# The final norm taken by token, on rows turned ahead of the norm

## The chip, the core and the metric

One core of one Trainium2 chip runs the kernel. TensorE multiplies matrices into PSUM (eight banks of 128 partitions by 512 fp32), VectorE and ScalarE work on PSUM and SBUF, SyncE and ScalarE issue the transfers used here. The metric is the device time of one execution in microseconds (us); runs are compared by their median.

## The reference

A decoder layer on 512 tokens of width 1024: a SwiGLU feed-forward block, a token mixer (gMLP gating and a Mamba-2 scan), a second feed-forward block, a gated per-layer embedding, and a final norm, all fp32. The change lies in the last two steps:

```python
def rmsnorm(x, g):
    xf = x.astype(jnp.float32)
    y = xf * lax.rsqrt(jnp.mean(xf * xf, axis=-1, keepdims=True) + EPS)
    return (y * g.astype(jnp.float32)).astype(x.dtype)
...
        h = h + 0.5 * swiglu(rmsnorm(h, ffn2_norm[i]), ffn2_w_gate[i], ffn2_w_up[i], ffn2_w_down[i])
        gate = jax.nn.sigmoid(rmsnorm(h, ple_norm[i]) @ ple_w_gate[i] + ple_b_gate[i])
        h = h + gate * (p[i] @ ple_w_proj[i])
    return rmsnorm(h, final_norm)
```

## The kernel before

The residual `h` is kept as 8 tiles of 128 features (on the partitions) by 512 tokens, `h[0]` to `h[7]`. A product of fp32 operands is made in three passes: `weights(src, n)` loads 1024 columns of weights (`raw`), ScalarE casts them to fp32r (`whi`), VectorE subtracts to get the rest (`wlo`), and `accumulate` multiplies `whi` and `wlo` with the two parts of the activations `x`, 8 x 3 matmuls for each tile of 128 outputs.

The last stage has one such unit for each d from 0 to 7, called here the product of d. Units 0 to 4 are multiplied with all 512 tokens; units 5, 6 and 7 (`BY_HALF = 3`) with the first 256 tokens and the last 256 separately (`gate_half`). The norm's factor `r` for the tokens comes from the sums of squares of `h` (matmuls with `ones`, a root by Newton steps on VectorE, `diagonals`, and `spread`, a matmul that copies the factor to all partitions; `kept` is ScalarE's copy of it). `gate` then makes four steps for each d: a multiply by `r` (VectorE, from PSUM), a sigmoid (ScalarE), a multiply by the embedding tile `emb[d]` (VectorE), an add to `h[d]` (VectorE). After it each `h[d]` is squared (ScalarE; VectorE for d = 7), the full-width squares are added into `total`, and `gained` multiplies `h[d]` by the final norm's vector, one number for each feature, that is for each partition.

The output wants tokens on rows. For each half of the tokens `factors` sums the squares with matmuls by `ones` and takes the root (`rsqrt_by_table`: ScalarE's Sqrt, VectorE's reciprocal and one Newton step), and `rows_out` turns `h` by 128 x 128 transposes into PSUM, four to a tile (a tile holds 128 tokens by 512 features), scales each tile by the token's factor into `o` and stores it: ScalarE scales the first 512 features, VectorE the other 512, eight stores of 256 KB in all.

The program is recorded first and issued in an order that is written out by hand: `ORDER` is a list of unit numbers, where a unit is one instruction, or the matmuls in a row into one PSUM tile. Every engine works through its own instructions in this order, and waits for others by semaphores. PSUM tiles come from seven banks of the tag `b` and one of `a`. In the profile nearly all instructions carry the line of the call that issues them (L1905), so rows are told apart by tile names.

The part of `ORDER` that concerns the end lists TensorE's work as: the products of d = 1 and 0 (full), the sums, d = 2, the spread, d = 4, 5 (first half), 3, 5 (second half), 6 (first, second), 7 (first, second), the ones products of the first half, four of the turned tiles, the ones products of the second half, four turned tiles.

Of the kernel before, what the change touches and what calls it, by code (L numbers as in the profile page):

```python
# [27 lines left out]
ALU = mybir.AluOpType  # L28
# [24 lines left out]
    "m": 33, "convin": 2, "o": 8, "sq": 4,  # L53
}
REGION = dict.fromkeys(("raw0", "s0", "embt", "F", "xfa", "xfb", "x", "xa", "xb", "r4", "u", "emb"), "left") | dict.fromkeys(
    ("rawb", "whix", "wlox", "s1", "rawd", "ghi", "glo", "g", "u2", "p7", "m", "convin", "o", "sq"), "right",
# [15 lines left out]
    ("ple_b_gate", 8), ("final_norm", 8), ("d_skip", 8),  # L72
# [4 lines left out]
for _name, _w in _VECS:  # L77
# [211 lines left out]
def layer_kernel(ctx: ExitStack, tc: tile.TileContext, a: dict, out: bass.AP):  # L289
# [96 lines left out]
    def tmp():  # L386
        return sb("tmp")
# [1410 lines left out]
    def gate(d, ps, tok, engine):  # L1798

        t = tmp()[:, tok]  # L1800
        nc.vector.tensor_tensor(t, ps[:, tok], r[:, tok], ALU.mult)
        nc.scalar.activation(t, t, AF.Sigmoid, bias=col("ple_b_gate", d))
        engine.tensor_tensor(t, t, emb[d][:, tok], ALU.mult)
        engine.tensor_tensor(h[d][:, tok], h[d][:, tok], t, ALU.add)
        sq = tmp() if tok is whole else sb("sq", (P, half))
        if d < ND - 1:
            nc.scalar.activation(sq, h[d][:, tok], AF.Square)
        else:
            nc.vector.tensor_tensor(sq, h[d][:, tok], h[d][:, tok], ALU.mult)
        return sq  # L1810

    def gained(d, tok):

        if d < ND - 1:
            nc.scalar.activation(h[d][:, tok], h[d][:, tok], AF.Copy, scale=col("final_norm", d))
        else:
            nc.vector.tensor_scalar(
                h[d][:, tok], h[d][:, tok], col("final_norm", d), None, ALU.mult
            )

    total = sb("ssum")

    def done(d, ps):
        sq = gate(d, ps, whole, nc.vector)
        if d == 0:
            nc.vector.tensor_copy(total, sq)
        else:
            nc.vector.tensor_tensor(total, total, sq, ALU.add)
        gained(d, whole)

    for d in range(ND - BY_HALF):
        ps = mm_ps()
        accumulate(ps, weights(a["ple_gate"][d], D), 0, x)
        if d == 0:
            tok, first = norm.per_token(D), ps
            continue
        if d == 1:
            r = Norm.on_all(tok)
            done(0, first)
        done(d, ps)  # L1840
    units = [weights(a["ple_gate"][d], D) for d in range(ND - BY_HALF, ND)]
    def gate_half(i, tok):
        d = ND - BY_HALF + i
        ps = sm_ps()
        accumulate(ps[:, tok], units[i], 0, x, tokens=tok)
        sq = gate(d, ps, tok, nc.vector)
        gained(d, tok)
        return sq

    def factors(tok, sqs):  # L1850

        chunks = range(tok.start // P, tok.stop // P)
        ps = sm_ps()
        for j, sq in enumerate([total[:, tok]] + sqs):
            for i in range(len(chunks)):
# [157 lines left out]
```

## Time and profile before

| | |
|---|---|
| median of 3 runs | 1073.28 us (1072.68 to 1074.14) |
| profiled execution | 1073.36 us, of which the span is 1071.6 us |
| granted TensorE clock, mean over the span | 0.999 |
| TensorE matmuls busy | 1062.1 us (99% of the span) |
| VectorE busy | 817.0 us (76%) |
| ScalarE busy | 559.5 us (52%) |
| GpSimd busy | 75.2 us (7%) |
| HBM traffic | 161 GB/s over the span |

Times in the views count from the span's start. A row of the timeline has the start, the duration, the engine (PE is TensorE, PEld its weight load, DVE VectorE, ACT ScalarE, SP SyncE; a q behind the name is the engine's queue of DMA issues), the line, the operation, what it writes <- what it reads, shapes, and how many are merged (x3); in brackets stands how long the engine was idle before it, and what ended the wait.

### The profile page before, as it was taken

How to read it: one execution, taken by the hardware profiler on the slowest of the kernel's cores; microseconds unless marked ns; L12 is line 12 of the kernel's file. 1: busy time of each engine (PE TensorE's matmuls, PEld its weight loads, DVE VectorE, ACT ScalarE, POOL GpSimd, SP SyncE). 2: the span in 40 equal slices, each digit the busy share in tenths (PEclk: the TensorE clock that was granted, in tenths of full speed). 3: DMA queues.
4: the chain of work that ended last, by engine and by line, in shares of the span. 5: the costliest groups of instructions: out<-in, count | busy, mean ns of one | idle time of the engine just before them, and what ended most of it. 6: DMA issues, size and time to landing. Idle time of an engine off the chain costs nothing.

```text
span 1071.6 us, 17611 instructions
## 1 busy us (share of the span) xinstructions
PE 1062.1 (99%) x7151; PEld 965.0 (90%) x7151; DVE 817.0 (76%) x1169; ACT 559.5 (52%) x781; POOL 75.2 (7%) x95
## 2 busy tenths in 40 slices
PE   9999999999999999999999999999999999999997
PEld 7899999999998878998999888999999999999887
DVE  6978685867577879999999767988667575857866
ACT  7655344444444537887865435654434343534545
POOL 1100000100000000000100000010100000000000
PEclk9999999999999999999999999999999999999999
DMA  9876765766452236777855435786755757633412
GB/s 322 238 202 166 196 181 193 196 181 174 99 154 82 65 113 146 187 201 175 212 135 130 138 98 137 218 236 186 204 143 155 211 144 197 181 115 85 139 53 79
DMA packets 52209, 173.27 MB, mean 162 GB/s; under 512 B 5920, under 2 KB 6176, under 8 KB 52128
## 3 DMA queue, kind: packets, MB, share of 16 engines
q1 hardware_dynamic: 33696, 116.93, 32.1%
q0 software_dynamic: 12256, 44.57, 23.1%
q10 hardware_dynamic: 6176, 10.65, 3.4%
q8 instruction: 56, 0.92, 0.3%
q14 instruction: 25, 0.20, 0.1%
HBM read 167.86 MB, written 4.26 MB: 161 GB/s over the span
## 4 chain that ended last, share of the span: by engine, by line
PE 99%; DVE 0%; ACT 0%; issue 0%; DVEq 0%; ACTq 0%
PE b L1905 81%; PE a L1905 18%; DVEq L2008 0%; DVE o L1905 0%; ACT m L1905 0%; ACT b L1905 0%; DVE tmp L1905 0%; DVE h L1905 0%; DVE ones L410 0%; DVE nv L1905 0%; ACTq L1905 0%
## 5 line engine op out<-in xcount | busy, mean ns | idle before, releaser
L1905 PE MATMUL b<-xfb,whi 128*128 128x256 f32 (+1 forms) x1704 | 297.5, 278 | 0.7 <-ACT b L1905 0.7
L1905 PEld LDWEIGHTS b<-xfb,whi 128*128 128x128 f32 x1704 | 261.0, 188 | 6.0 <-ACT b L1905 0.9
L1905 PE MATMUL b<-xfb,wlo 128*128 128x256 f32 (+1 forms) x852 | 237.2, 278 | 0.0
L1905 ACT CAST whi<-raw 128x1024 fp32r<-128x1024 f32 (+1 forms) x131 | 136.0, 1041 | 146.4 <-PE b L1905 109.7
L1905 DVE TENSOR_TENSOR wlo<-raw,whi 128x1024 fp32r<-128x1024 f32 (+1 forms) x130 | 156.8, 1212 | 28.7 <-ACT whi L1905 25.8
L1905 PEld LDWEIGHTS b<-xfb,wlo 128*128 128x128 f32 x852 | 159.9, 188 | 0.5
L1905 PE MATMUL b<-xfa,whi 128*128 128x256 f32 (+1 forms) x696 | 124.0, 281 | 0.0
L1905 PEld LDWEIGHTS b<-xfa,whi 128*128 128x128 f32 x696 | 107.0, 188 | 2.5 <-DVE xfa L1905 0.2
L1905 PE MATMUL b<-xfa,wlo 128*128 128x256 f32 (+1 forms) x348 | 97.8, 281 | 0.0
L1905 ACT CAST whix<-rawd 128x1024 fp32r<-128x1024 f32 (+1 forms) x40 | 39.4, 986 | 88.5 <-PE a L1905 47.9
L1905 DVE TENSOR_TENSOR wlo<-rawb,whi 128x1024 fp32r<-128x1024 f32 x51 | 62.1, 1220 | 23.2 <-ACT whi L1905 23.1
L1905 ACT CAST whi<-rawb 128x1024 fp32r<-128x1024 f32 x51 | 53.3, 1049 | 48.8 <-PE b L1905 39.7
L1905 PE MATMUL b<-m,whi 128*128 128x512 f32 x224 | 69.6, 392 | 0.0
L1905 DVE TENSOR_TENSOR wlox<-rawd,whix 128x1024 fp32r<-128x1024 f32 (+1 forms) x40 | 45.7, 1143 | 27.0 <-ACT whix L1905 26.9
L1905 PEld LDWEIGHTS b<-xfa,wlo 128*128 128x128 f32 x348 | 65.4, 188 | 0.5
L1905 PE MATMUL b<-xb,whi 128*128 128x256 f32 (+1 forms) x280 | 62.2, 318 | 0.0
L1905 PE MATMUL b<-ghi,wlox 128*128 128x512 f32 x156 | 61.4, 394 | 0.0
L1905 PE MATMUL b<-glo,whix 128*128 128x512 f32 x156 | 61.2, 392 | 0.0
L1905 PE MATMUL b<-ghi,whix 128*128 128x512 f32 x156 | 60.7, 389 | 0.0
L1905 PE MATMUL a<-ghi,wlox 128*128 128x512 f32 x140 | 55.2, 394 | 0.0
L1905 PE MATMUL a<-glo,whix 128*128 128x512 f32 x140 | 54.9, 392 | 0.0
L1905 PE MATMUL a<-ghi,whix 128*128 128x512 f32 x140 | 54.4, 389 | 0.0
(294 smaller groups left out, 2223.8 us busy)
## 6 DMA issues: line engine op xcount, KB each, us to landing
raw<-in_ffn_gu SPq DMA_DIRECT2D x57, 512.0 KB, 5.4
rawd<-in_ffn_down SPq DMA_DIRECT2D x40, 512.0 KB, 4.4
raw<-in_ffn_gu POOLq DMA_DIRECT2D x32, 512.0 KB, 7.7
rawb<-in_ffn_gu SPq DMA_DIRECT2D x31, 512.0 KB, 6.1
s<-in_ffn_gu SPq DMA_DIRECT2D x21, 512.0 KB, 5.5
s<-in_ffn_gu POOLq DMA_DIRECT2D x21, 512.0 KB, 8.5
raw<-in_w_out SPq DMA_DIRECT2D x16, 512.0 KB, 3.6
raw<-in_w_in SPq DMA_DIRECT2D x13, 512.0 KB, 3.7
```

Source lines behind the costliest of these rows:

```text
L1905: getattr(getattr(real, engine), what)(*(real_of(x) for x in args), **{k: real_of(x) for k, x in kw.items()})
```

## The change

The squares, totals and gains on `h` go, and so do `factors` and `rows_out`. `h` is turned first, without the final norm's vector. ScalarE squares the turned tiles in PSUM along the row and sums them in the same instruction (`accum_out`), in three parts: the first 512 features, the next 384 and the last 128. The final norm's vector is loaded once to all partitions as rows (`fn`, 128 x 1024), and VectorE applies it to the turned tiles. For the first half one VectorE instruction scales by the factor and by `fn`; for the second half the first 512 features are multiplied by `fn` ahead of the factor (`upper`) and scaled by ScalarE after it. The first half takes its root by Newton steps on VectorE, the second by ScalarE's Sqrt, whose first use on a constant stands ahead of the real one.

```diff
-    ("ple_b_gate", 8), ("final_norm", 8), ("d_skip", 8),
+    ("ple_b_gate", 8), ("d_skip", 8),
...
+    fn = sb("fn", (P, D))
+    nc.scalar.dma_start(fn, a["fn"].partition_broadcast(P))
+    class Rows:
...
+        def turn(self, q, part=slice(0, 4)):
+            for i, c in enumerate(self.chunks):
+                if (q, i) not in self.ps:
+                    self.ps[q, i] = mm_ps()
+                ps = self.ps[q, i]
+                for d in range(part.start, part.stop):
+                    nc.tensor.transpose(chunk(ps, d), chunk(h[4 * q + d], c), ident)
+        def squares(self, q, part, n):
+            for i in range(2):
+                w = slice(part.start * P, part.stop * P)
+                nc.scalar.activation(
+                    sb("junk")[:, w], self.ps[q, i][:, w], AF.Square, accum_out=self.ss[n][:, i : i + 1]
+                )
+        def upper(self):
+            for i in range(2):
+                self.o[0, i] = sb("o")
+                nc.vector.tensor_tensor(self.o[0, i], self.ps[0, i], fn[:, :T], ALU.mult)
+        def so_far(self):
+            self.e = sb("ssq", (P, 2))
+            nc.vector.tensor_tensor(self.e, self.ss[0], self.ss[1], ALU.add)
+            if self.half:
+                nc.vector.tensor_scalar(self.e, self.e, 1.0 / D, EPS, ALU.mult, ALU.add)
+        def out(self):
+            rt = sb("rlast", (P, 2))
+            if self.half:
+                v, y, t = (sb(n, (P, NC))[:, :2] for n in ("nv", "ny", "nt"))
+                nc.vector.scalar_tensor_tensor(v, self.ss[2], 1.0 / D, self.e, ALU.mult, ALU.add)
+                nc.scalar.activation(y, v, AF.Sqrt)
...
+            else:
+                v = sb("ssq", (P, 2))
+                nc.vector.tensor_tensor(v, self.ss[2], self.e, ALU.add)
+                rsqrt(rt, v, 1.0 / D, (P, 2))
+            for i, c in enumerate(self.chunks):
+                rows = out[c * P : (c + 1) * P]
+                if self.half:
+                    o = self.o[0, i]
+                    nc.scalar.activation(o, o, AF.Copy, scale=rt[:, i : i + 1])
+                else:
+                    o = sb("o")
+                    nc.vector.scalar_tensor_tensor(
+                        o, self.ps[0, i], rt[:, i : i + 1], fn[:, :T], ALU.mult, ALU.mult
+                    )
+                (nc.scalar if self.half else nc.sync).dma_start(rows[:, :T], o)
+                o = sb("o")
+                nc.vector.scalar_tensor_tensor(o, self.ps[1, i], rt[:, i : i + 1], fn[:, T:], ALU.mult, ALU.mult)
+                nc.sync.dma_start(rows[:, T:], o)
...
+    rows = [Rows(i) for i in range(2)]
+    for row in rows:
+        row.turn(0)
+        row.squares(0, slice(0, 4), 0)
+        if row.half:
+            row.upper()
...
+    for tok, row in zip(halves, rows):
+        for i in range(BY_HALF - 1):
+            gate_half(i, tok)
+        row.turn(1, slice(0, 3))
+        row.squares(1, slice(0, 3), 1)
+        row.so_far()
+        gate_half(BY_HALF - 1, tok)
+        if row.half:
+            nc.scalar.activation(sb("ssq", (P, 2)), ones[:, 0:2], AF.Sqrt)
+        row.turn(1, slice(3, 4))
+        row.squares(1, slice(3, 4), 2)
+        row.out()
```

`ORDER` is written anew for the end; elsewhere a handful of units move by a place. Read by engine, with A for the first half of the tokens and B for the second, 0 and 1 for the two row tiles of a half, `up` for the first 512 features, `lo3` for the next 384 and `lo1` for the last 128:

```text
TensorE: products d=1, d=0, sums, d=4, d=3, spread, d=2, then halves 5A 7A 6A 6B 5B,
         turns up A1, up A0, lo3 A1, lo3 A0, lo1 A0, lo1 A1, up B1, product 7B,
         turns up B0, lo3 B1, lo3 B0, lo1 B0, lo1 B1
ScalarE: ... sigmoids d0 d3 d2 d1 d4 6A 5A 7A 6B 5B, squares up A1, lo3 A1, up A0, lo3 A0, lo1 A0, lo1 A1,
         up B1, sigmoid 7B, squares up B0, lo3 B0, lo3 B1, lo1 B1, lo1 B0, Sqrt of a constant, Sqrt of B,
         scale up B1, store, scale up B0, store
VectorE: ... add 6B, upper B1, so_far A, add 5B, first 8 steps of A's root, multiply by r of 7B, 1 step,
         2 steps, multiply by emb of 7B, last step, add 7B, o lo A1, so_far B, o up A0, so_far B (second),
         o lo A0, v of B, o up A1, reciprocal and Newton step of B, o lo B1, o lo B0, upper B0
```

In this order the turn into the last quarter (`lo1`) of A's lower tiles is listed ahead of the square that reads their first three quarters (`lo3`); for B it is listed behind it. Of the loads of `emb`, those of d = 1 and 4 now stand ahead of ScalarE's last two casts of the feed-forward block's gate values, and the load of `fn` stands behind the cast of unit 2.

More of the change, by code (lines that the diff above doesn't have):

```diff
@@ L52 @@
     "whix": 1, "wlox": 1, "s1": 2, "rawd": 2, "ghi": 3, "glo": 3, "g": 1, "u2": 1, "p7": 1,
-    "m": 33, "convin": 2, "o": 8, "sq": 4,
+    "m": 33, "convin": 2, "o": 8, "ssq": 10, "fn": 1, "t": 6, "junk": 2,
 }
 REGION = dict.fromkeys(("raw0", "s0", "embt", "F", "xfa", "xfb", "x", "xa", "xb", "r4", "u", "emb"), "left") | dict.fromkeys(
-    ("rawb", "whix", "wlox", "s1", "rawd", "ghi", "glo", "g", "u2", "p7", "m", "convin", "o", "sq"), "right",
+    ("rawb", "whix", "wlox", "s1", "rawd", "ghi", "glo", "g", "u2", "p7", "m", "convin", "o", "fn", "t", "junk", "ssq"), "right",
 )
@@ L1796, in layer_kernel, with gate @@
     whole, halves = slice(0, T), (slice(0, half), slice(half, T))
-    def gate(d, ps, tok, engine):
-        t = tmp()[:, tok]
+    def gate(d, ps, tok):
+        t = sb("t")[:, tok]
         nc.vector.tensor_tensor(t, ps[:, tok], r[:, tok], ALU.mult)
         nc.scalar.activation(t, t, AF.Sigmoid, bias=col("ple_b_gate", d))
[L1803 to L1829, printed above, removed]
+        nc.vector.tensor_tensor(t, t, emb[d][:, tok], ALU.mult)
@@ new lines, in gate, with __init__ @@
+        nc.vector.tensor_tensor(h[d][:, tok], h[d][:, tok], t, ALU.add)
+    fn = sb("fn", (P, D))
+    nc.scalar.dma_start(fn, a["fn"].partition_broadcast(P))
+    class Rows:
+        def __init__(self, half):
+            self.half = half
+            self.chunks = range(half * (NC // 2), (half + 1) * (NC // 2))
+            self.ss = [sb("ssq", (P, 2)) for _ in range(3)]
+            self.ps, self.o = {}, {}
+        def turn(self, q, part=slice(0, 4)):
[26 more added lines that the diff above has]
+                nc.scalar.activation(y, v, AF.Sqrt)
+                nc.vector.reciprocal(y, y)
+                nc.vector.tensor_tensor(t, y, y, ALU.mult)
+                nc.vector.scalar_tensor_tensor(t, t, -0.5, v, ALU.mult, ALU.mult)
+                nc.vector.scalar_tensor_tensor(rt, t, 1.5, y, ALU.add, ALU.mult)
+            else:
[16 more added lines that the diff above has]
+                nc.sync.dma_start(rows[:, T:], o)
@@ L1838, in layer_kernel @@
             r = Norm.on_all(tok)
-            done(0, first)
-        done(d, ps)
+            gate(0, first, whole)
+        gate(d, ps, whole)
     units = [weights(a["ple_gate"][d], D) for d in range(ND - BY_HALF, ND)]
+    rows = [Rows(i) for i in range(2)]
[4 more added lines that the diff above has]
+            row.upper()
     def gate_half(i, tok):
@@ L1845, in gate_half @@
         accumulate(ps[:, tok], units[i], 0, x, tokens=tok)
[L1846 to L1855, printed above, removed]
-                nc.tensor.matmul(
-                    ps[:, i : i + 1], sq[:, i * P : (i + 1) * P], ones[:, 0:1], start=i + j == 0,
-                    stop=j == len(sqs) and i == len(chunks) - 1, skip_group_check=True,
-                )
-        rt = sb("rlast", (P, 2))
-        rsqrt_by_table(rt, ps[:, :2], 1.0 / D, (P, 2))
-        return rt
-    def rows_out(tok, rt):
-        for i, c in enumerate(range(tok.start // P, tok.stop // P)):
-            for q in range(2):
-                ps = mm_ps()
-                for d in range(4):
-                    nc.tensor.transpose(chunk(ps, d), chunk(h[4 * q + d], c), ident)
-                o = sb("o")
-                if q == 0:
-                    nc.scalar.activation(o, ps, AF.Copy, scale=rt[:, i : i + 1])
-                else:
-                    nc.vector.tensor_scalar(o, ps, rt[:, i : i + 1], None, ALU.mult)
-                (nc.sync if q else nc.scalar).dma_start(out[c * P : (c + 1) * P, q * T : (q + 1) * T], o)
-    squares_of = [[], []]
-    for i in range(BY_HALF):
-        squares_of[0].append(gate_half(i, halves[0]))
-    for i in range(BY_HALF):
-        if i == BY_HALF - 1:
-            r_a = factors(halves[0], squares_of[0])
-        squares_of[1].append(gate_half(i, halves[1]))
-    rows_out(halves[0], r_a)
-    rows_out(halves[1], factors(halves[1], squares_of[1]))
+        gate(d, ps, tok)
+    for tok, row in zip(halves, rows):
[10 more added lines that the diff above has]
+        row.out()
     homes["psum"].open(psum)
@@ L1983, in _laid_out @@
     o["gm_w"] = np.ascontiguousarray(one["gm_w_s"].transpose(2, 0, 1).reshape(P, 8 * P))
+    o["fn"] = one["final_norm"].reshape(1, D)
     o["gm_b"] = one["gm_b_s"].reshape(1, 8 * P)
```

90 rows, old and new, of the table ORDER are left out of this document.

## The prediction

> **What bounds the kernel now.** I read the page first, then the chain of waits for the last 72 us, then the timeline of the last 20 us, then the stores of the output one by one.
>
> ```profile
> span 1071.6 us, 17611 instructions
> ## 1 busy us (share of the span) xinstructions
> PE 1062.1 (99%) x7151; PEld 965.0 (90%) x7151; DVE 817.0 (76%) x1169; ACT 559.5 (52%) x781; POOL 75.2 (7%) x95
> ```
>
> TensorE is busy for 99% of the span: up to the last product only less TensorE work, or a hole in it, can move the time. The chain says where that rule stops:
>
> ```profile
> 1005.54 57.18 PE b L1905 x346
> ...
> 1065.87 0.66 DVE o L1905
> ```
>
> One unbroken TensorE piece runs from 1005.5 to 1062.7; behind it the chain hops between engines and ends in a VectorE write of an output tile. The change edits this tail. Its rows, from the timeline (start, duration, engine, operation):
>
> ```profile
> 1054.69 0.43 DVE L1905 TENSOR_TENSOR tmp<-b,rall 128x256 f32<-128x256 f32 x1 [1.79 <-PE b L1905]
> ...
> 1057.25 0.28 PE L1905 MATMUL b<-x,wlo 128*128 128x256 f32 x1
> ...
> 1057.61 0.42 DVE L1905 TENSOR_TENSOR tmp<-b,rall 128x256 f32<-128x256 f32 x1
> ...
> 1058.06 0.51 ACT L1905 ACTIVATE tmp<-tmp,vec 128x256 f32<-128x256 f32 x1 [1.52 <-DVE tmp L1905]
> 1058.47 0.71 ACT L1905 ACTIVATE h<-h,vec 128x512 f32<-128x512 f32 x1
> 1058.60 0.43 DVE L1905 TENSOR_TENSOR tmp<-tmp,emb 128x256 f32<-128x256 f32 x1 [0.57 <-ACT tmp L1905]
> 1058.97 1.82 PEld L1905 LDWEIGHTS b<-ident,h 128*128 128x128 f32 x16
> 1059.08 1.95 PE L1905 MATMUL b<-ident,h 128*128 128x128 f32 x16
> 1059.19 1.28 ACT L1905 ACT_TABLE_LOAD   x1
> 1059.25 0.16 DVE L1905 TENSOR_SCALAR nv<-b 128x2 f32<-128x2 f32 x1 [0.23 <-PE b L1905]
> 1059.33 0.75 DVE L1905 TENSOR_TENSOR h<-h,tmp 128x256 f32<-128x256 f32 x2
> ...
> 1060.49 0.20 ACT L1905 ACTIVATE ny<-nv 128x2 f32<-128x2 f32 x1
> 1060.60 0.40 ACT L1905 ACTIVATE sq<-h 128x256 f32<-128x256 f32 x1
> ...
> 1064.45 2.07 DVE L1905 TENSOR_SCALAR o<-b,rlast 128x512 f32<-128x512 f32 x3 [0.53 <-PE b L1905]
> ```
>
> The last half-wide product (unit 7, second half of the tokens) ends at 1057.5. Its gate (multiply, sigmoid, multiply, add) ends at 1059.75, the first of the two adds at 1059.33. Ones products, the root, the turns and three output tiles follow, and the last tile is written at 1064.45 + 2.07 = 1066.5. What is left is the stores (the view of the tile `out`, for three moments):
>
> ```profile
> L1905 SPq DMA_DIRECT2D out<-o x2: 333/505/677, 1066.5 to 1066.9; - x2
> DMA to landing us min/median/max: 2.9/3.0/3.1
> ...
> DMA to landing us min/median/max: 2.1/2.1/2.1
> ```
>
> The last store is issued at 1066.9 and lands 3.1 later, at 1070.0; 1.6 more end the span at 1071.6. The fastest of the eight took 2.1. The profiled execution took 1073.36 us, 1.8 around its span; the median of the runs is 1073.28, so the sum may be put on 1073.3.
>
> **Durations.** Four more rows, from the timelines of VectorE and ScalarE:
>
> ```profile
> 1024.30 0.15 DVE L1905 TENSOR_TENSOR nt<-ny 128x4 f32<-128x4 f32 x1
> 1024.49 0.16 DVE L1905 SCALAR_TENSOR_TENSOR nt<-nt,nv 128x4 f32<-128x4 f32 x1
> ...
> 1037.08 1.89 DVE L1905 TENSOR_TENSOR h<-h,tmp 128x512 f32<-128x512 f32 x3
> ...
> 1013.01 1.66 ACT L1905 ACTIVATE tmp<-h 128x512 f32<-128x512 f32 x3
> ```
>
> On VectorE a tiny operation takes 0.195 of the queue (1024.49 - 1024.30); a half-wide one 0.33 (two in 0.75, each 0.42 long); a full one 0.60 (three in 1.89, each 0.69 long); a scaled output tile 0.66 (three in 2.07, each 0.75 long). On ScalarE a full Square takes 0.53 (three in 1.66, each some 0.6 long). A half-wide one is 0.40 long, so by a straight line three quarters take 0.42 of the queue and a quarter 0.21. A 128x128 turn takes 1.82/16 = 0.114 of TensorE; a half-wide product 2.92 (1057.61 - 1054.69).
>
> **The change, part by part.**
>
> *Early moves.* Some loads of `emb` go ahead of two casts on ScalarE, the second FFN's last products swap a place, one 512 KB load (`fn`) joins ScalarE's queue, and the product of d=2 goes behind the spread of the norm. Each stands beside a busy TensorE. The spread comes one full product later, so five whole gates queue on VectorE at once: 15 operations of 0.60, 9.0 us, of which all but those of the half products must be through before the first turn. From the spread to that turn there are one full product and five halves, some 7 x 2.92 = 20 us, and in them VectorE also splits two units and gates four halves; they fit. I price all this at nothing. Were that cover gone, TensorE would wait before the turns one for one; bounds 0 to +0.5.
>
> *Removed.* ScalarE and VectorE lose all full and half squares, the totals and the gains (hidden under products: worth nothing there). TensorE loses the ones products, 1.7 us for each half (1057.25 to 1058.97 for the first), but they stood behind the last product, in the tail.
>
> *TensorE's new order.* The written order puts 16 turns of the first half and 4 of the second ahead of the last half-product: 20 x 0.114 = +2.3. That product now ends at 1057.5 + 2.3 = 1059.8, and its gate could begin at 1059.9 instead of 1057.6.
>
> *The wait that I think decides.* VectorE's queue holds, ahead of that gate, `upper` on the second half's second tile (row tile 3 of the output), which multiplies by `fn` a PSUM tile that ScalarE squares too. Do two engines read one PSUM tile side by side? The kernel has one such place:
>
> ```profile
> 400.25 0.27 PE L1905 MATMUL b<-ident,acs 128*64 128x128 f32 x1
> 400.56 0.28 DVE L1905 COPY csrow<-b 64x128 f32<-64x128 f32 x1 [0.58 <-PE b L1905]
> 400.77 1.52 DVE L1905 SCALAR_TENSOR_TENSOR m<-convin,vec,m 128x510 f32<-128x510 f32 x2
> 400.88 0.27 ACT L1905 ACTIVATE csrow<-b 64x128 f32<-64x128 f32 x1 [4.09 <-DVE csrow L1905]
> ```
>
> ScalarE had been idle for 4.09 us and the tile was complete at 400.52, yet it starts at 400.88, just after VectorE's copy (400.56 + 0.28 = 400.84), though the two only read the tile and write different halves of `csrow`. So I let `upper` wait for the square. The Trainium skill, page "PSUM — Partial Sum Buffer", section "PSUM bank collisions raise a hardware error", says the same: the compiler puts a dependency between instructions of two engines on one bank and quadrant, reads included. By that rule the sum is the one below; without it, the first rival's.
>
> *The squares with their sum.* No row shows the accumulating form. Below it: nothing extra; above it: one more tiny ScalarE instruction of full length, 0.20. I take 0.11, the room such an instruction takes (1060.49 to the next start at 1060.60), as the sum must be read out somewhere; both ends go into the range.
>
> *The sum.* Unit 5's second half is the last product ahead of the turns, so it comes out where unit 7's first half did: its multiply at 1054.69, its sigmoid ends 0.43 + 0.51 later with the hand-over, at 1055.66. Then ScalarE's squares: the first at 1055.66; the second is listed behind the last quarter's turn into its PSUM tile (turns from 1054.5 on, 16 x 0.114, so 1056.4) and starts at 1056.5. From there 0.42 + 0.53 + 0.42 + 0.21 + 0.21 + 0.62 for the six up to the second half's first, plus 6 x 0.11: 1059.55. On VectorE: `upper` 0.60, `so_far` 0.20, the held-up add 0.33, eight tiny ones of the first half's root 1.56: the last gate begins at 1062.25, not at 1059.9. Its four steps (0.42, 0.51, 0.43 and 0.42, with hand-overs and one tiny operation between) end at 1064.2. Before it was 1059.75: +4.4.
>
> Behind that add, ScalarE, which had the sigmoid until 1063.2, squares one full tile and two of three quarters (0.64 + 0.53 + 0.53), then two quarters (0.31 each, behind the turn): 1065.8. Then the table load 1.28 and the first root: free at 1067.25. VectorE meanwhile writes three tiles of the first half (3 x 0.66) and three tiny ones up to 1066.9, and a fourth tile up to 1067.5, so recip starts at 1067.5: the load is just covered by the tiles. Four tiny operations, 0.78: 1068.3. Then two output tiles, 2 x 0.66, and only then `upper` of the other tile, 0.69: 1070.3. ScalarE scales that tile, 0.7: the last tile is written at 1071.05, against 1066.5: +4.5. So the tail behind the add is as long as before (6.85 against 6.8): what the ones products gave is spent on squares, the table load behind them, four first-half tiles and the late `upper`.
>
> *Stores.* The last one is issued at 1071.05, where it was 1066.9: +4.15. Four of the first half went earlier, so it shares the queues with two at most: between 2.1 and 3.1 to land, I take 2.5 (nearer the uncrowded row), -0.6: 1073.55, + 1.6 = 1075.15 against 1071.6. **Sum: +4.15 - 0.6 = +3.6 on 1073.3: 1076.9 us.**
>
> **Rivals.**
>
> *The two readers do not wait.* `upper` would then run at 1056.7 in an idle queue and the gate begin at 1059.9. Not all of the 2.3 comes back, as ScalarE's squares in the tail are then the late ones: add 1062.2, last tile about 1.8 earlier, 1075.1; with free accumulation some 0.8 less, 1074.3. For it: both only read. Against it: the `csrow` rows. 0.17, within 0.2% (2.15 us, about what a measurement of this kernel can tell from no change).
>
> *Costlier still.* Accumulation at 0.20 gives 11 x 0.09 = 1.0 over the six squares ahead of `upper` and the five in the tail, of which some 0.9 shows: 1077.8, inside the main case. A hole in TensorE from the early moves adds up to 0.5. The Trainium skill ("ScalarE: Activation LUTs", section "What ACT_TABLE_LOAD costs") adds a drain of 1.38 us to each load; by it the second half's root would come 1.3 later, 1078.2. The trace does not agree: load 1059.19 + 1.28 = 1060.47, root at 1060.49. Above 1078.4: 0.10.
>
> *Faster.* The other side needs the first half to be through before the last gate, so that VectorE's queue is empty behind it and ScalarE can load the root's table behind the last sigmoid, under the add and the turns. The first half's root (12 tiny, 2.3) and four tiles (2.6) would have to lie ahead of 1059.9, so begin at 1055.0, with the gate of unit 7's first half just done. Then the tail is gate 1.95, turns 0.25, two quarter squares 0.6, root 1.2 (tiny operations and the table's), two tiles on each engine 1.4: last tile at 1065.3; store 2.1 and 1.6: 1069.0, or 1070.7 us by the run. It decides only if the first half's squares end by 1055; by the steps above they end near 1058.5, and the written order puts the last gate ahead of that root's end and the load behind the last square. 0.05.
>
> *The change does nothing measurable in the tail* because the stores set the end: eight stores in the same stretch. But the last tile must be written before its store goes, and that is 4.5 later. 0.02.
>
> **How the numbers follow.** Main case 0.66, from 1075.6 (free accumulation -0.9, 2.1 to land -0.4) to 1078.4 (0.20: +0.9, 3.1: +0.6): nearly all slower; 0.04 of it falls within 0.2%, should the waits also be shorter than I put them. Slower (above 1075.4): 0.62 + 0.10 = 0.72; same: 0.17 + 0.04 + 0.02 = 0.23; faster 0.05. The range takes in the first rival and the main case, 1074.2 to 1078.6, and leaves out 0.15; the main case's own is 1075.6 to 1078.4.
>
> **What would show it.** The last half-product ends 2.3 later; `upper` (o from b and fn) starts only when a ScalarE square ends; the multiply of the last gate starts some 2 us after its product ends, with VectorE busy; behind the tail's last square the table load; the very last tile is ScalarE's, behind a VectorE multiply by `fn`; the first half's factor is ready later than before. I am wrong if that multiply starts within 0.3 of its product, if TensorE shows a hole before the turns, or if a square costs much more than its width.

## The result, and the profile after

The kernel after takes 1089.49 us (median of 4 runs, 1088.88 to 1090.07), the kernel before, run beside it, 1073.70 us: a ratio of 1.0148, 95% interval 1.0131 to 1.0166. That is 12.6 us above the forecast and outside its range. The page of the kernel after, and its row in the list of cores:

```profile
span 1087.9 us, 17547 instructions
## 1 busy us (share of the span) xinstructions
PE 1072.3 (99%) x7119; PEld 973.9 (90%) x7119; DVE 816.9 (75%) x1174; ACT 554.7 (51%) x785; POOL 75.2 (7%) x95
```

```profile
core 0: 1087.9 us, clock 0.996
```

TensorE has 32 instructions less (the ones products) and is busy 10.2 us longer: it is still 99%. No hole in it explains the loss: ahead of the last product its pauses come to 1.7 us, where they came to 0.9 in the kernel before. Nor does the clock. Its mean fell from 0.999 to 0.996, but in stretches it stands at 1.00 in both kernels up to the tail, and in the kernel after the low part (0.50) lies behind 1080 us, where TensorE has nothing left to do. In the chain of waits the kernels can be laid side by side, piece by piece. First before, then after:

```profile
48.19 13.61 PE b L1905 x120
...
71.44 8.22 PE b L1905 x60
...
81.05 13.61 PE b L1905 x120
```

```profile
48.25 13.61 PE b L1928 x120
...
71.48 8.40 PE b L1928 x60
...
81.24 14.14 PE b L1928 x120
```

A piece is an unbroken run of products into PSUM, here in the first feed-forward block (FFN); up products are its products by the gate and up weights, down products those by the down weights. The first piece, 120 up products, is alike in both kernels. The last takes 14.14 us instead of 13.61, for the same 120 up products on the same shapes: 117.8 ns each instead of 113.4. The piece of 60 ahead of it, which holds 48 up products, already takes 8.40 instead of 8.22. The loss starts some 72 us into the kernel, nearly a millisecond ahead of anything that the new norm does. The groups by line with shapes kept apart say which products are slower (busy us, mean ns of one). Before:

```profile
L1905 PE MATMUL b<-xfb,whi 128*128 128x256 f32 x1680 | 290.0, 277 | 0.7 <-ACT b L1905 0.7
...
L1905 PE MATMUL b<-m,whi 128*128 128x512 f32 x224 | 69.6, 392 | 0.0
...
L1905 PE MATMUL b<-ghi,wlox 128*128 128x512 f32 x156 | 61.4, 394 | 0.0
```

After:

```profile
L1928 PE MATMUL b<-xfb,whi 128*128 128x256 f32 x1680 | 298.9, 281 | 0.7 <-ACT b L1928 0.7
...
L1928 PE MATMUL b<-m,whi 128*128 128x512 f32 x224 | 70.9, 398 | 0.0
...
L1928 PE MATMUL b<-ghi,wlox 128*128 128x512 f32 x156 | 61.0, 391 | 0.0
```

The FFNs' up products (xfa, xfb) and the mixer's output products (m) got slower, the down products (ghi, glo with whix, wlox) a little faster. Summing the distances from one product's start to the next over the trace, without the few long pauses, gives +12.1 us for 3524 up products (402.0 to 414.1), +2.4 for 382 of m (87.2 to 89.6), and -1.7 for 888 down products (203.9 to 202.2).

What in the change reaches so far? One line that I quoted and did not price: `final_norm` leaves the table `_VECS`, so `vec` has 172 columns instead of 180. By the rounding of the places this moves every later tile of the base pool and of the left regions down by 32 bytes in each partition. The right regions stay.

### The profile page after: what moved, and what is told of

Its sections match the earlier page's. It is cut to its first block, busy times and chain, and to the rows that moved or that the text cites. A ratio compares the mean times of both kernels' runs of the same rounds, so it can differ in the third digit from the quotient of the medians.

```text
span 1087.9 us, 17547 instructions
## 1 busy us (share of the span) xinstructions
PE 1072.3 (99%) x7119; PEld 973.9 (90%) x7119; DVE 816.9 (75%) x1174; ACT 554.7 (51%) x785; POOL 75.2 (7%) x95
## 4 chain that ended last, share of the span: by engine, by line
PE 97%; ACT 1%; DVE 1%; DMA 1%; issue 0%; SPq 0%; DVEq 0%; ACTq 0%
PE b L1928 80%; PE a L1928 17%; DMA h<-in_x 1%; ACT junk L1928 0%; ACT xfa L1928 0%; DVE o L1928 0%; ACT ghi L1928 0%; ACT L1928 0%; DVE xfa L1928 0%; SPq L1928 0%; DVE nt L1928 0%; ACT whi L1928 0%; ACT o L1928 0%; DVEq L2032 0%; ACT m L1928 0%
## 5 line engine op out<-in xcount | busy, mean ns | idle before, releaser
L1928 PE MATMUL b<-xfb,whi 128*128 128x256 f32 (+1 forms) x1704 | 306.5, 283 | 0.7 <-ACT b L1928 0.7
L1928 PEld LDWEIGHTS b<-xfb,whi 128*128 128x128 f32 x1704 | 264.8, 190 | 5.8 <-ACT b L1928 0.9
L1928 PE MATMUL b<-xfb,wlo 128*128 128x256 f32 (+1 forms) x852 | 240.8, 283 | 0.0
L1928 PE MATMUL b<-xfa,whi 128*128 128x256 f32 (+1 forms) x696 | 127.5, 285 | 0.2 <-DVE xfa L1928 0.2
```

Source lines behind the costliest of these rows:

```text
L1928: getattr(getattr(real, engine), what)(*(real_of(x) for x in args), **{k: real_of(x) for k, x in kw.items()})
```

## The experiments

Addresses below are bytes in a partition, from the placement of the built programs. In the kernel before whi, wlo, xfa and xfb lie at multiples of 64, in the kernel after 32 bytes past one; the FFNs' right regions (ghi, glo, whix, wlox) are 32 bytes past one in both.

**1. Eight unused columns put back.**

```diff
-    ("dt_bias", 16), ("a_log", 16),
+    ("dt_bias", 16), ("a_log", 16), ("spare", 8),
```

> The kernel after, with eight unused columns put back at the end of the table of vectors, so that every tile of the base pool and of the left regions lies again at the byte address that it had before (a multiple of 64). Nothing else differs. Theory A (the 13.8 us ahead of the tail come from the narrower table, which moved these tiles by 32 bytes): the 13.8 us go, the tail's own +2.5 us stay: 1075 to 1077 us. Theory B (the granted clock, 0.996 against 0.999, some 3 us) or theory C (the new order, the load of the norm's vector, the rows' instructions): the time stays near 1089 us.

Measured: 1076.28 us, ratio 1.0024 (1.0014 to 1.0034), a mean granted clock of 0.996 as in the kernel after. Theory A holds, B and C fall: 13.2 us go with the addresses. The chain's piece is that of before again:

```profile
81.13 13.61 PE b L1928 x120
```

**2. The kernel before, its table eight columns wider.** The same line in the kernel before.

> The kernel before, with eight unused columns more in its table of vectors: all of its own work and order, but base and left tiles 32 bytes further, at 32 modulo 64. Theory A: slower by the same 12 to 14 us, 1085 to 1088 us, the spacing of the products of xfb and whi up from 114 to 118 ns. Theories B and C: 1073.7 us, no change.

Measured: 1085.09 us, ratio 1.0106 (1.0091 to 1.0121). The old kernel, with its old tail, is made slow by 32 bytes alone (the same piece of the chain):

```profile
81.37 14.13 PE b L1905 x120
```

**3. Sixteen columns wider.**

> The kernel before with sixteen unused columns more: the same tiles moved by 64 bytes, again at multiples of 64. If what counts is the address modulo 64: 1073 to 1074.5 us. If any move of these tiles costs, or a wider table does: as slow as with eight columns more, about 1086 us.

Measured: 1075.64 us, ratio 1.0017 (1.0008 to 1.0026). The up products keep the quick pace (114.0 ns); but those of m went to 234.6 ns, so 64 bytes aren't free either. No cost of a wider table as such shows.

**4. The left regions alone moved back.**

```diff
-PAD = {"sb": 0, "ffn_left": 384, "mix_left": 384, "ple_left": 448, ...
+PAD = {"sb": 0, "ffn_left": 416, "mix_left": 416, "ple_left": 480, ...
```

> The kernel after with the left regions alone moved up by 32 bytes (the moving operands xfa, xfb, xa, xb and x at multiples of 64 again), while the base pool with the weights' high and low parts stays at 32 modulo 64. If the moving operand's address decides: 1075 to 1077 us. If the stationary operand's (whi, wlo) decides: near 1089 us. If each adds its share: between, about 1082 us.

Measured: 1094.29 us, ratio 1.0192 (1.0175 to 1.0209), slower than any theory gave. With the moving operands at multiples of 64 and the weights 32 past, the up products take 118.5 ns. So neither operand's own address decides alone; I turned to distances between tiles.

**5. The mixer's right region 32 bytes lower, in the kernel after** (`"mix_right": 96` to `128`).

> The kernel after with the mixer's right region alone moved down by 32 bytes, so that its tiles m (moving operand of the mixer's output products) lie again at the same address as whi and wlo modulo 512; both are then at 32 modulo 64. Theory A1 (the distance between the moving and the stationary operand decides): the 512-wide products of m fall back from 235 to 227-229 ns, some 380 of them, -2.4 us, all others stay: 1086.5 to 1087.5 us. Theory A2 (the operand's own address modulo 64 decides): m leaves a multiple of 64, its products stay at 235 ns or get slower: 1089.5 us or more.

Measured: 1087.23 us, ratio 1.0122 (1.0106 to 1.0137): -2.3 us, as theory A1 says. m's products run at 228.3 ns whenever m and the weights have the same address modulo 512 (before, and here at 32 past a multiple of 64), at 234.6 at each of the three other distances that occurred (32, 448, 480). (These means take in two pauses; the medians are 227 and 233 to 234.) The 512-wide products of `x` in the last stage agree: their median is 227 in the eight kernels in which x and whi have the same address modulo 512, and 234 in that of experiment 4, where they stand 32 bytes apart.

**6. The FFNs' right regions 32 bytes lower, in the kernel before** (`"ffn_right": 0` to `32`).

> The kernel before with the FFNs' right regions alone moved down by 32 bytes: ghi, glo and whix, wlox keep their distance to each other (0 modulo 512) and go from 32 to 0 modulo 64, where the base pool and the left regions are. Spacings before: 230 to 232 ns in three of these four groups, where the kernel after has 227. If these groups are slow because their region and the base pool differ modulo 64: -2 us, and the products of ghi and glo with whi (distance 96 before, 64 now) -0.8 us: 1070.5 to 1072 us. If only the distance within a pair counts: 1073 to 1074 us.

Measured: 1083.09 us, ratio 1.0084 (1.007 to 1.0098): 9 us slower, where I expected a gain or nothing. Neither operand of an up product was moved, yet those slowed down; the down products, whose tiles were moved together, got faster (groups by line, shapes kept apart):

```profile
L1905 PE MATMUL b<-xfb,whi 128*128 128x256 f32 x1680 | 299.3, 281 | 0.7 <-ACT b L1905 0.7
...
L1905 PE MATMUL b<-ghi,wlox 128*128 128x512 f32 x156 | 60.7, 389 | 0.0
```

So the pace of the up products goes with where the FFNs' right region, which holds the tiles of the down products that run between them, stands against their own tiles. That was a new theory (A3). The region holds other tiles too (weights as loaded, values on their way to ghi and glo); they moved with it, and no run tells them apart from the tiles of the down products.

**7. The fourth corner: the kernel after, narrow table and all, with its right regions moved** (`"ffn_right": 32`, `"mix_right": 128`).

> The kernel after with its narrow table, and only the right regions moved down by 32 bytes: the FFNs' (ghi, glo, whix, wlox) to 0 modulo 64, the mixer's (m) to the same address as whi modulo 512. Base and left stay at 32. Theory A3 (what matters is that the up products' operands and the right region's stand at different halves of 64 bytes, as in the kernel before): the products of xfa and xfb run at 113 to 114 ns, 1076 to 1077 us, as with the eight spare columns. Theory A2 (operands at 32 modulo 64 are slow by themselves): they stay at 117 to 118 ns, and only m's gain is left: about 1087 us.

Measured: 1075.40 us, ratio 1.0024 (1.0015 to 1.0034). A3 holds, and this undoes the loss without a spare column (the same piece):

```profile
81.30 13.61 PE b L1928 x120
```

The runs together; places modulo 64, m's distance from whi modulo 512, mean ns from start to start:

| kernel | up operands | FFN right | m - whi | up | down | m | us |
|---|---|---|---|---|---|---|---|
| before | 0 | 32 | 0 | 114.1 | 229.6 | 228.3 | 1073.7 |
| after | 32 | 32 | 32 | 117.5 | 227.6 | 234.6 | 1089.5 |
| 1, after, 8 spare | 0 | 32 | 0 | 114.1 | 229.6 | 228.3 | 1076.3 |
| 2, before, 8 spare | 32 | 32 | 480 | 117.7 | 226.6 | 234.6 | 1085.1 |
| 3, before, 16 spare | 0 | 32 | 448 | 114.0 | 228.7 | 234.6 | 1075.6 |
| 4, after, left moved | 0 and 32 | 32 | 32 | 118.5 | 227.3 | 234.6 | 1094.3 |
| 5, after, m moved | 32 | 32 | 0 | 117.7 | 227.6 | 228.3 | 1087.2 |
| 6, before, right moved | 0 | 0 | 0 | 117.7 | 226.6 | 228.3 | 1083.1 |
| 7, after, right moved | 32 | 0 | 0 | 114.1 | 229.7 | 228.3 | 1075.4 |

Up products are quick where their operands and the FFNs' right region stand in different halves of 64 bytes, slow where in the same half; the down products the other way round. Experiment 4, whose two operands stand in different halves, is a case of its own: 118.2 to 118.4 ns in every stretch.

The traces of these nine kernels also show where the pace is chosen. Each has 51 unbroken runs of 24 to 144 up products that begin right behind a down product. In the four quick kernels all 51 keep 113.3 ns, and in the four slow ones all 51 keep 117.8. The eight runs that begin behind another product (all between 35 and 740 us) don't follow this: in each of these eight kernels some of them are quick and some slow.

**8 and 9. Is it the address, or a pace that the chain falls into?** In the kernel after the first run of up products is quick (48.25 above) with the same tiles that are slow later. So I disturbed the chain by 28 narrow products at the head of up tiles, in the kernel after and in that of experiment 1. (They fell into both FFNs, at some 200 to 310 and 680 to 945 us, not into the first alone as the text on record says.)

```diff
+                    if fresh and p == m == 0:
+                        KICK[0] += 1
+                        if 12 < KICK[0] <= 40:
+                            n = 32 * (1 + KICK[0] % 7)
+                            nc.tensor.matmul(
+                                o[:, :n], whi[:, c], xhi[:, :n], start=True, stop=False, skip_group_check=True
+                            )
```

> The kernel after with 28 extra narrow products (32 to 224 columns, about 60 ns each, 1.7 us in all) ahead of the first product of some up tiles of the first FFN; each is overwritten by the product behind it. Theory P (addresses do not choose the pace; the moment at which a product happens to start does, and the pace is kept until something shifts it): one of the seven widths throws the chain from 117.5 back to 113.5 ns, for tens of us: below 1086 us. Theory A (addresses choose): each kick is forgotten within a few products: 1089.5 + 1.7 = 1091 us.

> The kernel after with eight spare columns and the same 28 extra narrow products. Theory P: some kick throws the chain from 113.5 to 117.5 ns for tens of us: 1080 us or more. Theory A: 1076.3 + 1.6 = 1078 us, the pace of the products behind a kick again 113 to 114 ns.

Measured: 1091.52 us (2 runs) and 1080.23 us (2 runs). A kick costs more than I allowed: about 112 ns whatever its width (one of 32 columns took 32 ns and the product behind it 203, one of 224 took 105 and 125, where a product alone takes 118), so some 3.1 us for the 28. So 1076.3 + 3.1 and 1089.5 + 3.1 are the times to compare with: both kernels kept their pace by and large, as theory A says. The trace gives theory P a share. Timeline of TensorE around one kick (a product of 128 columns), in the kernel after with kicks; the rows are every third product:

```profile
265.54 0.28 PE L1936 MATMUL b<-xfa,wlo 128*128 128x256 f32 x1
...
265.90 0.28 PE L1936 MATMUL b<-xfa,wlo 128*128 128x256 f32 x1
266.01 0.51 PE L1936 MATMUL b<-xfa,whi 128*128 128x128 f32 x3
...
267.40 0.28 PE L1936 MATMUL b<-xfa,wlo 128*128 128x256 f32 x1
...
267.74 0.28 PE L1936 MATMUL b<-xfa,wlo 128*128 128x256 f32 x1
```

The same kick in the kernel of experiment 1:

```profile
261.72 0.28 PE L1936 MATMUL b<-xfa,wlo 128*128 128x256 f32 x1
...
262.06 0.28 PE L1936 MATMUL b<-xfa,wlo 128*128 128x256 f32 x1
262.17 0.51 PE L1936 MATMUL b<-xfa,whi 128*128 128x128 f32 x3
...
263.23 0.28 PE L1936 MATMUL b<-xfa,wlo 128*128 128x256 f32 x1
...
263.58 0.28 PE L1936 MATMUL b<-xfa,wlo 128*128 128x256 f32 x1
```

In the first, three products take 0.36 us ahead of the kick and 0.34 behind it: quick, at the addresses called slow. In the second it is the other way round, 0.34 ahead and 0.35 behind (by the trace's starts 113.3 and 117.7 ns a product). Such a spell lasts as long as the run of up products that it falls into, 24 to 120 of them or 3 to 14 us; of the 84 runs that begin behind a down product without a kick, 83 are at the kernel's own pace again. So both paces occur at either placement, a run keeps the one that it starts with unless a kick throws it, and the addresses go with the one that it takes up behind a down product. What in the chip holds the two paces apart no run here shows.

**10. The tail: the wait taken off VectorE.** On the kernel of experiment 1, in the written order:

```diff
-... 2698 2644 2659 2693 2669-2676 2706 2677 ...
+... 2698 2659 2693 2669-2676 2706 2644 2677 ...
```

Unit 2644 is the second tile's `upper`, 2706 the last gate's multiply.

> The kernel after with the eight spare columns (1076.3 us), and in the written order VectorE's multiply of the second half's second tile by the norm's vector stands directly behind the last gate's first multiply instead of ahead of the first half's totals. If that multiply, which waits for ScalarE's square of the same PSUM tile, is what holds the last gate (theory of the prediction): the gate begins at 1060.3, held only by the tiny operations, and 1.3 to 1.8 us go: 1074.5 to 1075.0 us. If ScalarE's squares or the table's load set the tail whatever the gate does: 1076.3 us.

Measured: 1075.52 us, ratio 1.0014 (1.0005 to 1.0023), between the two. Timeline:

```profile
1060.10 0.60 PE L1934 MATMUL b<-ident,h 128*128 128x128 f32 x4
...
1060.62 0.42 DVE L1934 TENSOR_TENSOR t<-b,rall 128x256 f32<-128x256 f32 x1
...
1066.73 0.16 DVE L1934 SCALAR_TENSOR_TENSOR rlast<-nt,ny 128x2 f32<-128x2 f32 x1
...
1067.37 1.41 DVE L1934 SCALAR_TENSOR_TENSOR o<-b,rlast,fn 128x512 f32<-128x512 f32 x2 [0.48 <-DVE rlast L1934]
...
1069.41 0.72 ACT L1934 ACTIVATE o<-o,rlast 128x512 f32<-128x512 f32 x1 [1.77 <-DVE o L1934]
```

Counted from the turns behind the last product, the gate begins 0.52 later, where experiment 1 has 2.11 (below): the wait is gone. Of these 1.6 us the factor `rlast` keeps 1.24 and the last tile 0.87. Between the two lies a pause of 0.48 on VectorE, where experiment 1 has 0.11; its named releaser had ended when it began, and what it waits for stays open.

**11. The tail reordered:** both `upper`s ahead of ScalarE's squares of the same tiles, so that ScalarE waits and not VectorE; all first-half turns ahead of the last half-product; the root's table loaded behind the last sigmoid and one square. The last units of `ORDER` (addresses as in experiment 1):

```diff
+... 2639 2643 2658 2657 2668 2659 2669 2670 2705 2642 2671 2672 2673 2641 2674 2675 2676 2699 2677 2678
+2706 2679 2701 2680 2683 2707 2687 2708 2700 2709 2702 2710 2703 2712 2684 2685 2688 2704 ...
```

> The kernel after with the eight spare columns and another written order of the last 100 units: both multiplies by the norm's vector ahead of ScalarE's squares of the same PSUM tiles (so that ScalarE waits, not VectorE), all turns of the first half and the first upper tiles of the second ahead of the last half-product, the table of the root loaded straight behind the last sigmoid. By this run's own durations the last gate's multiply then begins at 1060.3, and the last tile is written at 1067.2 instead of 1070.6: 1072.5 to 1073.5 us. If the squares with their read-outs fill ScalarE and set the tail by their sum: no gain, 1076 us.

Measured: 1074.90 us, ratio 1.0008 (0.9999 to 1.0017): some 40% of the gain that I expected. Timeline:

```profile
1061.12 0.82 PE L1934 MATMUL b<-ident,h 128*128 128x128 f32 x6
...
1061.50 0.42 DVE L1934 TENSOR_TENSOR t<-b,rall 128x256 f32<-128x256 f32 x1
...
1063.17 1.28 ACT L1934 ACT_TABLE_LOAD   x1
...
1067.07 1.33 ACT L1934 ACTIVATE o<-o,rlast 128x512 f32<-128x512 f32 x2 [1.11 <-DVE rlast L1934]
1067.14 1.41 DVE L1934 SCALAR_TENSOR_TENSOR o<-b,rlast,fn 128x512 f32<-128x512 f32 x2
1068.43 0.85 ACTq L1934 DMA_DIRECT2D out<-o  x2
```

The last tile comes 7.4 us behind the last product (1068.55 - 1061.12) instead of 10.9. But the last product is later by 0.5 for four more turns ahead of it (0.9 more it was late in this execution before the tail began), and four stores leave almost at once: 1073.5 - 1068.55 = 4.95 us follow the last tile to the end of the span, against 1074.2 - 1070.6 = 3.6 in experiment 1.

**12. The candidate: that order, with 24 spare columns and m back at whi's address modulo 512** (`"mix_right": 32`).

> A candidate: the reordered tail (1074.9 us), with 24 spare columns instead of eight (the operands at the places that gave 1075.6 us with the kernel before's order) and the mixer's right region 64 bytes higher, so that m and whi stand again at the same address modulo 512. From the sixteen-column run of the kernel before: +1.9 us for the move, of which 2.3 us were the products of m (366 of them, 6.3 ns each), now given back: 1074.0 to 1075.0 us, level with the kernel before. If the pace falls into the slow kind: 1085 us.

Measured: 1073.43 us, ratio 1.0003 (0.9994 to 1.0012): level with the kernel before, 16 us under the kernel after. No version here beats the kernel before.

## Why the prediction was wrong, and where it was right

The failed step is the first sentence behind the page: up to the last product "only less TensorE work, or a hole in it, can move the time". The time moved by 13.2 us (1089.49 against experiment 1's 1076.28) with neither: the same products, without a hole, came at another pace. With that sentence as a screen I went over the diff for work added or removed, "*Early moves*", priced at nothing, and gave the line that takes eight columns from the table no term at all, not even a bound. Its bound could not have been read off the profile of before as a sum of durations. But that profile did hold a warning: one and the same product came at both paces, 0.36 us for three at 36 us, 0.34 at 48 us, so the pace was a quantity that could change:

```profile
36.15 0.28 PE L1905 MATMUL b<-xfa,wlo 128*128 128x256 f32 x1
...
36.51 0.28 PE L1905 MATMUL b<-xfa,wlo 128*128 128x256 f32 x1
...
48.26 0.28 PE L1905 MATMUL b<-xfb,wlo 128*128 128x256 f32 x1
...
48.60 0.28 PE L1905 MATMUL b<-xfb,wlo 128*128 128x256 f32 x1
```

The rest, the tail, can be judged on experiment 1, which has the new tail on the old addresses. There the forecast was 1076.9 and the time is 1076.28. The nearness is in part luck: as a difference it is +2.5 us on the kernel before run beside it (1073.77), where the forecast was +3.6 on 1073.3. The two terms that I put too long are the last tile, by 0.45, and its store, by 0.4. The row of the kernel before that the first point starts from:

```profile
1057.37 0.50 PE L1905 MATMUL b<-ones,ssum 128*128 128x1 f32 x4
```

The timeline of experiment 1:

```profile
1054.64 2.35 PE L1928 MATMUL b<-ident,h 128*128 128x128 f32 x20
...
1059.08 0.24 ACT L1928 ACTIVATION_READ_ACCUMULATOR junk<-b 128x1 f32 x1
...
1059.35 0.69 DVE L1928 TENSOR_TENSOR o<-b,fn 128x512 f32<-128x512 f32 x1 [2.29 <-ACT junk L1928]
...
1059.70 1.23 PE L1928 MATMUL b<-ident,h 128*128 128x128 f32 x7
...
1061.81 0.42 DVE L1928 TENSOR_TENSOR t<-b,rall 128x256 f32<-128x256 f32 x1
...
1063.27 0.43 DVE L1928 TENSOR_TENSOR h<-h,t 128x256 f32<-128x256 f32 x1
...
1065.35 1.28 ACT L1928 ACT_TABLE_LOAD   x1
1066.65 0.20 ACT L1928 ACTIVATE ssq<-ones 128x2 f32<-128x2 f32 x1
...
1069.88 0.72 ACT L1928 ACTIVATE o<-o,rlast 128x512 f32<-128x512 f32 x1 [1.40 <-DVE o L1928]
1070.64 0.34 ACTq L1928 DMA_DIRECT2D out<-o  x1
```

- *The last half-product* 2.3 later: the turns behind it start at 1059.70, where the ones products started at 1057.37. Right.
- *The wait of `upper`*: it starts at 1059.35, just behind the read-out of ScalarE's square of its tile (1059.08 + 0.24), after 2.29 us idle; forecast 1059.55. Right, and the trace agrees with the rule that the Trainium skill states ("PSUM — Partial Sum Buffer", "PSUM bank collisions raise a hardware error"). The first rival (readers don't wait) falls.
- *The last gate* begins at 1061.81, forecast 1062.25; its add ends at 1063.70, forecast 1064.2. Experiment 10 shows that the wait was the cause.
- *The squares' sums*: a ScalarE instruction of its own, 0.19 to 0.24 long, which holds up the next by 0.09 to 0.10. I had 0.11; the bound of 0.20 and the costlier rival fall. So does the drain behind the table load: the load ends at 1066.63 and the next instruction starts at 1066.65.
- *The last tile* is written at 1070.60, forecast 1071.05, by ScalarE behind VectorE's multiply, as forecast. *Its store* takes 2.1 to land, the lower end, where I took 2.5. Thus a span of 1074.2 instead of 1075.15.
- *The faster rival*, a table load under the add, is built in part by experiment 11: there the load runs beside the last gate's second multiply and its add, but the first half's output tiles are still written behind the gate's first step, not ahead of it as the rival asked. The last product had to wait for more turns, and the stores bunched. So its 1070.7 was not reached (1074.90), and, its condition met in part only, it was not tested.

In the kernel after the same tail stands 13.7 us later: the 20 turns begin at 1068.30, the last gate at 1075.46, the last tile ends at 1084.26.

## What to carry to other kernels

A change in the size of any tile that is placed early is a change of the address of all that come behind it: before pricing a diff, list which operands of the bounding engine it moves, and give that a range of its own, however small the line. When a time is off and the bounding engine is busy throughout, compare like pieces of the chain (so many products, so many us) from the front; the first pair that differs says where it starts, and here it was nearly a millisecond ahead of the new tail. Spare columns that keep the old places tell in one run whether the code or the placement did it.

## What the runs showed of the hardware that was not expected

- The same 256-column product chain on TensorE runs at one of two paces, 113.3 and 117.8 ns a product (118.2 to 118.4 throughout in experiment 4), and keeps it from one product to the next; an extra product of any of several widths can throw it from one to the other, in either direction. 512-column products of m take 227 or 234 ns (medians).
- Which pace is taken behind a down product goes with places in SBUF that 32 bytes change: 51 of 51 runs at 117.8 instead of 113.3 ns, 1085.1 against 1073.8 us for the kernel before with and without eight spare columns. The Trainium skill ("SBUF — State Buffer", "Who interferes with whom") gives TensorE two independent read ports and names only the pair that VectorE shares with GpSimd as contended. Taken alone, that rule gives no reason for these moves to cost anything; the runs show up to 18 us (1094.3 against 1076.3). Whether a port is involved is open.
- An extra 32-column product costs the chain some 112 to 117 ns, about as much as one of 224 columns: its own 32 ns, and 203 instead of 118 for the product behind it.
